# Seven block products for eight in the gates and in most of the down projection of a gated decoder layer

## The chip, the cores and the metric

The kernel runs on one core of a Trainium2 chip. A core has TensorE (PE) for matmuls, VectorE (DVE), ScalarE (ACT) and GpSimd (POOL) for elementwise work, and SyncE (SP), whose queue issues nearly all of this kernel's transfers to 16 DMA engines. The metric is the device time of one execution in microseconds; the median of several runs is given. Where a number comes from the profile, it is from one profiled execution.

## The reference, cut to what matters

One decoder layer on 2048 prompt positions and 64 sample positions, D = 1024, all in float32:

```python
h = rms_norm(x, pre_mix_g)
z = h @ w_in                                   # q, k, v, sg_u, sg_v, mq, gate_logits (3 x 1024)
branches = stack([attn, sg, memo])             # three branches of width 512
proj = einsum('blnc,ncd->blnd', branches, w_o)
gates = sigmoid(gate_logits.reshape(B, L, 3, 1024))
x = x + rms_norm(sum(gates * proj, axis=2), post_mix_g)
up = rms_norm(x, pre_ffn_g) @ w_up             # 1024 -> 2 * 2816
c = conv_b + sum(ext[:, j:j + L] * conv_w[j] for j in range(3))
act = gelu(gate half of c) * (value half of c)
x = x + rms_norm(act @ w_down, post_ffn_g)     # 2816 -> 1024
```

Beside the layer's output the caches and states are returned. The change touches what starts with `gate_logits` and ends with the down projection.

## The kernel before

Everything lies with channels on the 128 partitions and tokens along the free axis. The 2112 tokens form three groups of T2 = 704 columns (NG2 = 3), each of two chunks of CW = 352. Matmul operands are split (`split`, L72 and L73) into a high part in the fast float32 format and a low part that is the rest: ScalarE casts, VectorE subtracts. Each product is three passes (`PASSES`): high x high, high x low, low x high.

`stage1` computes the three branches and writes them to DRAM (`br`), as well as the scale of each token (`rbc_d`). `stage2` has three phases.

The mix phase (L789) goes over the three groups. `build_h` loads x, scales and splits it into eight operand tiles. `proj0` computes the group's first branch. `branches` then goes over the three branches n and four pairs of output tiles: per output tile 48 gate matmuls in `gemm` (L741, tile `ps_g`), a sigmoid (L872), and for n = 1 and 2 also 24 matmuls of the projection (tile `ps_p`), a product (L877) and a sum on GpSimd (L878). `SumSq` adds squares. After a group, the projection of the next group's first branch is issued, then `post_mix`: the norm of the sum (`rstd_rows`, with tiny matmuls on both sides of a power on GpSimd), scaling, the residual, a store of x1, squares and the norm of x1 itself, stored as `rs2_d` (L897).

After each pair of output tiles `prep` (L801) is called, for 22 up weight tiles in all: it loads four 128x512 blocks of the weight (L809), forms four sums and differences of them (L816), splits each and stores it to `sum_d` (L819). It has pools of its own.

The up phase (L913) multiplies in quads: two output tiles by two chunks by two halves of the depth, as seven block products in place of eight. `build_ops` loads x1, scales it, forms four differences per depth pair and splits seven operands; 28 operand tiles stand in 32 buffers. `build_w` loads three weight blocks and splits them, and loads four prepared sums. Each product is 12 matmuls (L997) into one of three kinds of PSUM bank. The last product of a quad is issued after the first one of the next.

The down phase (L1102) takes six chunks of 352 columns. Each loads and splits its 22 activation tiles (L1117), and per output tile two halves of the weight (L1125), with 66 matmuls (L1141, tile `ps_d`). Then come the norm, the scaling and the residual.

The order on each engine is a schedule made when the program is built: it goes by the order of the program, but an instruction that has its inputs and its buffer may be put ahead. The queues are then served in that order. Pools of a phase take the memory of the phase before, tile by tile as it falls free.

Of the kernel before, what the change touches and what calls it, by code (L numbers as in the profile page):

```python
# [15 lines left out]
P = 128  # L16
# [26 lines left out]
def tile_decoder_layer(ctx, tc, I, O):  # L43
# [8 lines left out]
    rs2_d = dpool.tile([P, NTOK], F32, tag="rs2d", name="rs2_d")  # L52
    sum_d = [dpool.tile([4, P, 2, 512], F32, tag=f"sumd{f}", name=f"sum_d{f}") for f in range(NF)]
# [46 lines left out]
    stage2(tc, I, O, br, rbc_d, x1_d, rs2_d, act_d, sum_d, gains, split, PASSES, rstd_rows)  # L100
# [609 lines left out]
def stage2(tc, I, O, br, rbc_d, x1_d, rs2_d, act_d, sum_d, gains, split, PASSES, rstd_rows):  # L710
# [3 lines left out]
    with ExitStack() as c2:  # L714

        def pool(stack, name, bufs):
            return stack.enter_context(tc.tile_pool(name=name, bufs=bufs, reuse_waits="tile"))

        cm = c2.enter_context(ExitStack())
        hp, wp, lp, sp = pool(cm, "h2", 13), pool(cm, "w2", 4), pool(cm, "ld2", 2), pool(cm, "s2", 2)  # L720

        def psum(stack, name):
            return stack.enter_context(tc.tile_pool(name=name, bufs=3, space=PSUM, reuse_waits="tile"))

        ps2 = psum(cm, "ps2")

        def load_w(src, nm):
            w = wp.tile([P, 2, 1024], F32R, tag="w", name=f"w_{nm}")
            t = lp.tile([P, 1024], F32, tag="ws", name=f"ws_{nm}", bufs=2)
            nc.sync.dma_start(out=t, in_=src)  # L730
            split(w[:, 0], w[:, 1], t)
            return w.rearrange("p s (k c) -> p s k c", c=P)

        def gemm(w, ks, xs, nm, spare=False):

            ps = ps2.tile([P, 2, 512], F32, tag="st" if spare else "mm", name=f"ps_{nm}", bufs=1 if spare else 3)
            n, tot = 0, 3 * len(xs)
            for k, x in zip(ks, xs):
                for a, b in PASSES:
                    for c in range(2):  # L740
                        nc.tensor.matmul(  # L741
                            ps[:, c, :CW], lhsT=w[:, a, k], rhs=x[:, b, c * CW : (c + 1) * CW],
                            start=(n == 0), stop=(n == tot - 1),
                        )
                    n += 1
            return ps[:, :, :CW]
# [42 lines left out]
def mix_phase(c2, tc, env):  # L789
# [7 lines left out]
    with ExitStack() as ca:  # L797
# [3 lines left out]
        def prep():  # L801

            if not todo:
                return
# [487 lines left out]
```

## Time and profile before

| | |
|---|---|
| median of 3 runs | 3159.44 us (3154.03 to 3162.03) |
| the profiled execution | 3162.45 us |
| its span | 3160.7 us |
| TensorE busy | 2996.0 us (95%) |
| VectorE, ScalarE, GpSimd busy | 1821.8, 1329.4, 547.0 us |
| DMA moved | 566.88 MB, mean 179 GB/s |

The profiled execution's span is what the rows below divide up; 1.75 us lie around it. A busy time is the sum of an engine's instructions, with overlaps counted once. Matmuls overlap, so one that is listed with 323 ns follows the one before it at about half of that; the pieces of the chain show the real pace. The share of DMA is the mean busy share of 16 engines.

### The profile page before, as it was taken

The numbers are of one execution on the slowest core, as the hardware profiler recorded it, in microseconds if no ns is written. First come the engines' busy times: TensorE is split into PE (matmuls) and PEld (weight loads), VectorE is DVE, ScalarE is ACT, GpSimd is POOL, SyncE is SP. The second block draws the span as 40 slices with busy tenths as digits, with TensorE's granted clock in tenths as the row PEclk, the third lists the DMA queues.
The fourth block names the chain that finished last, engine by engine and source line by source line (L and its number), as shares of the span: only waits on it lengthen the run. The fifth ranks groups of instructions, "written<-read, shape, count | busy, mean of one in ns | idle before, by whom it ended". The sixth has DMA issues, their size and how long they took to land.

```text
span 3160.7 us, 51575 instructions
## 1 busy us (share of the span) xinstructions
PE 2996.0 (95%) x20060; PEld 2950.8 (93%) x20060; DVE 1821.8 (58%) x3061; ACT 1329.4 (42%) x2371; POOL 547.0 (17%) x662
## 2 busy tenths in 40 slices
PE   8999999998999699989994999999999997999997
PEld 8899999998999699979994999999999997999997
DVE  6665766546656832462228665865586655555552
ACT  5555565114333422332213444544454444444441
POOL 3221100000011301130113101311132210222221
PEclk9999999999999799989996999999999998999999
DMA  6222223218787832252217777777777757666652
GB/s 201 62 61 82 88 86 105 64 48 313 261 276 246 295 131 86 88 177 67 72 46 253 250 246 244 266 245 244 240 262 245 240 174 255 219 223 216 208 187 100
DMA packets 245268, 566.88 MB, mean 179 GB/s; under 512 B 30672, under 2 KB 103888, under 8 KB 245008
## 3 DMA queue, kind: packets, MB, share of 16 engines
q1 hardware_dynamic: 245024, 563.59, 53.5%
q8 instruction: 158, 2.59, 0.3%
q14 instruction: 86, 0.70, 0.1%
HBM read 459.35 MB, written 105.13 MB: 179 GB/s over the span
## 4 chain that ended last, share of the span: by engine, by line
PE 78%; DMA 8%; DVE 7%; issue 3%; ACT 2%; POOL 1%; SPq 0%; DVEq 0%; ACTq 0%; POOLq 0%
PE ps_d L1141 16%; PE ps_x L997 16%; PE ps_g L741 11%; PE ps_y L997 8%; PE ps_p L741 4%; PE ps_w L997 4%; PE ps_q L189 3%; PE ps_up L203 3%; PE ps_sv L189 3%; DMA pr<-in_w_dram 3%; PE ps_mqp L203 3%; DMA sum_d<-pw 2%; PE ps_kv L189 1%; DVE m L891 1%; DVE pw L73 1%
## 5 line engine op out<-in xcount | busy, mean ns | idle before, releaser
L741 PE MATMUL ps_g<-h,w_g 128*128 128x352 f32 x3456 | 574.1, 326 | 18.6 <-ACT m L855 18.6
L741 PEld LDWEIGHTS ps_g<-h,w_g 128*128 128x128 f32 x3456 | 566.3, 191 | 19.1 <-ACT m L855 19.1
L1141 PE MATMUL ps_d<-a,wd 128*128 128x352 f32 x3168 | 512.5, 323 | 17.8 <-ACT a L72 17.1
L1141 PEld LDWEIGHTS ps_d<-a,wd 128*128 128x128 f32 x3168 | 508.6, 189 | 19.1 <-ACT a L72 17.7
L741 PE MATMUL ps_p<-b,w_p 128*128 128x352 f32 x1728 | 291.4, 326 | 18.6 <-ACT w_p L72 13.0
L741 PEld LDWEIGHTS ps_p<-b,w_p 128*128 128x128 f32 x1728 | 283.2, 191 | 20.3 <-ACT w_p L72 13.4
L1065 DVE SCALAR_TENSOR_TENSOR c<-e,k_conv_w,c 128x704 f32<-128x704 f32 (+1 forms) x264 | 252.1, 956 | 68.8 <-ACT c L1061 61.7
L73 DVE TENSOR_TENSOR wd<-wr,wd 128x1408 fp32r<-128x1408 f32 x96 | 161.4, 1685 | 206.1 <-ACT wd L72 204.6
L997 PE MATMUL ps_x<-ot,ws 128*128 128x352 f32 x1584 | 277.5, 323 | 0.6 <-ACT p L1006 0.5
L997 PEld LDWEIGHTS ps_x<-ot,ws 128*128 128x128 f32 x1584 | 258.4, 189 | 1.9 <-ACT p L1006 1.0
L73 DVE TENSOR_TENSOR wa<-ra,wa 128x512 fp32r<-128x512 f32 x198 | 134.9, 689 | 155.5 <-ACT wa L72 154.7
L878 POOL TENSOR_TENSOR m<-m,sg 128x704 f32<-128x704 f32 x48 | 98.2, 2045 | 709.6 <-DVE sg L877 495.1
L72 ACT CAST wd<-wr 128x1408 fp32r<-128x1408 f32 x96 | 131.8, 1372 | 109.1 <-PE ps_d L1141 90.7
L872 ACT ACTIVATE sg<-ps_g 128x704 f32<-128x704 f32 x72 | 54.5, 756 | 284.4 <-PE ps_g L741 284.3
L1061 ACT ACTIVATE c<-e,k_conv_b,k_conv_w 128x704 f32<-128x704 f32 (+1 forms) x132 | 129.6, 982 | 68.8 <-DVE e L1031 49.0
L997 PE MATMUL ps_x<-ob,wa 128*128 128x352 f32 x792 | 147.3, 326 | 11.7 <-ACT wa L72 7.4
L72 ACT CAST wa<-ra 128x512 fp32r<-128x512 f32 x198 | 121.8, 624 | 85.9 <-PE ps_y L997 46.2
L73 DVE TENSOR_TENSOR w_g<-ws_g,w_g 128x1024 fp32r<-128x1024 f32 x72 | 98.7, 1371 | 91.9 <-ACT w_g L72 89.3
L1052 POOL COPY tails<-e 128x2 f32<-128x2 f32 x88 | 61.4, 697 | 520.6 <-DVE e L1031 520.4
L997 PE MATMUL ps_w<-ob,wa 128*128 128x352 f32 x792 | 147.9, 323 | 0.7 <-ACT wa L72 0.7
L997 PE MATMUL ps_y<-ot,ws 128*128 128x352 f32 x792 | 146.7, 324 | 0.3 <-DMA ws<-sum_d 0.3
L997 PEld LDWEIGHTS ps_x<-ob,wa 128*128 128x128 f32 x792 | 131.7, 191 | 12.5 <-ACT wa L72 7.6
(304 smaller groups left out, 5037.3 us busy)
## 6 DMA issues: line engine op xcount, KB each, us to landing
ws<-sum_d SPq DMA_DIRECT2D x264, 512.0 KB, 5.1
wr<-in_w_dram SPq DMA_DIRECT2D x96, 704.0 KB, 4.1
ra<-in_w_dram SPq DMA_DIRECT2D x198, 256.0 KB, 3.8
sum_d<-pw SPq DMA_DIRECT2D x88, 512.0 KB, 5.0
ws_g<-in_w_dram SPq DMA_DIRECT2D x72, 512.0 KB, 4.0
af<-act_d SPq DMA_DIRECT2D x132, 176.0 KB, 4.1
pr<-in_w_dram SPq DMA_DIRECT2D x88, 256.0 KB, 5.0
ws_p<-in_w_dram SPq DMA_DIRECT2D x36, 512.0 KB, 3.3
```

The source lines that it names most:

```text
L72: nc.scalar.copy(out=hi, in_=src)
L73: nc.vector.tensor_tensor(out=lo, in0=src, in1=_f(hi), op=ALU.subtract)
L189: nc.tensor.matmul(ps[:nt, :256], lhsT=h[k // 4][:, a, k % 4, c0 : c0 + nt], rhs=wv[:, b, k], start=(n == 0), stop=(n == 3 * KT - 1),)
L203: nc.tensor.matmul(ps[:, :nt], lhsT=wv[:, a, k, half * P : (half + 1) * P], rhs=h[k // 4][:, b, k % 4, :nt], start=(n == 0), stop=(n == 3 ...
L741: nc.tensor.matmul(ps[:, c, :CW], lhsT=w[:, a, k], rhs=x[:, b, c * CW : (c + 1) * CW], start=(n == 0), stop=(n == tot - 1),)
L872: nc.scalar.activation(v2(sg), ps, AF.Sigmoid)
L878: nc.gpsimd.tensor_tensor(out=mx[o], in0=mx[o], in1=sg, op=ALU.add)
L997: nc.tensor.matmul(ps[:, :CW], lhsT=self.ws[w][:, a, j], rhs=self.ops[o][j][:, b], start=(start and n == 0), stop=(n == 3 * HK - 1), skip_ ...
L1052: nc.gpsimd.tensor_copy(out=tails[:, ft], in_=e[:, T2 : T2 + 2])
L1061: nc.scalar.activation(c[:, :cwid], e[:, 2:ew], AF.Identity, bias=cb[:, ft : ft + 1], scale=cw[:, ft, 2:3])
L1065: nc.vector.scalar_tensor_tensor(out=c[:, :cwid], in0=e[:, t : t + cwid], scalar=cw[:, ft, t : t + 1], in1=c[:, :cwid], op0=ALU.mult, op1= ...
L1141: nc.tensor.matmul(ps[:, :CW], lhsT=w[:, a, k], rhs=acts[i * HF + k][:, b], start=(n == 0), stop=(n == 3 * NF - 1),)
```

## The change

The gates get a phase of their own ahead of the mix phase. It computes all 36 pairs of gate output tiles as quads of seven products, as the up phase does, and stores the sigmoids to DRAM (`sg_d`). In group 0 the sums of a gate weight are formed on the spot, used and stored; in groups 1 and 2 they are loaded. The up weights' sums are prepared there too, after each quad of groups 1 and 2 until the 22 are done, in the pools of the quads.

The mix phase then has the projections alone, and loads the gate tiles. `post_mix` of a group is issued after the second pair of output tiles of the next group. It stores the sums of squares of x1 (`acx_d`) in place of the finished norm; `norms` in the up phase makes the norm from them, for the next group at f = 8.

The down phase takes whole groups. 16 of the 22 depth tiles go in two batches of eight through seven-product quads that add into the output tiles `ys`; the other six go plainly (`plain`), and the norm and the residual of a group are held until after the next group's first quad. The eight down weights' sums are prepared in the up phase, one after each fourth quad. The quad code of the up phase has become the class `Strassen`, which all three phases use; `rw` has 10 buffers in the gate phase and 5 in the up phase as before, `wo` has 12 and in the down phase 10.

The diff's core:

```diff
+        def weights(self, w, sums, first, nm):
...
+            def total(i):
+                if ("s", i) not in raw:
+                    p, m, op = (
+                        (lambda: block(2), lambda: block(3), ALU.add),
+                        (lambda: block(0), lambda: block(2), ALU.subtract),
+                        (lambda: total(0), lambda: block(0), ALU.subtract),
+                        (lambda: block(1), lambda: total(2), ALU.subtract),
+                    )[i]
+                    p, m = p(), m()
+                    t = rw.tile([P, HK * P], F32, tag="raw", name=f"s{i}_{nm}")
+                    nc.vector.tensor_tensor(out=t, in0=p, in1=m, op=op)
+                    raw["s", i] = t
+                return raw["s", i]
...
+                t = wo.tile([P, 2, HK * P], F32R, tag="w", name=f"w{n}_{nm}")
+                if n[0] == "a":
+                    split(t[:, 0], t[:, 1], block(i))
+                elif first:
+                    split(t[:, 0], t[:, 1], total(i))
+                    nc.sync.dma_start(out=sums[i], in_=_f(t))
                 else:
+                    nc.sync.dma_start(out=_f(t), in_=sums[i])
...
+        def run(self, jobs):
+            prev = None
+            for nm, ws, ops, sink in jobs:
+                q = [nm, ws, ops, sink, {}]
+                p1 = self.copy(q, self.product(q, "x", "a11", "b11", True), "p1")
+                if prev:
+                    self.end(prev)
+                p5 = self.copy(q, self.product(q, "y", "s1", "t1", True), "p5")
+                sink.add(0, 0, p1, self.product(q, "w", "a12", "b21", True))
+                u2 = self.copy(q, self.product(q, "x", "s2", "t2", False), "u2")
+                sink.add(0, 1, u2, self.product(q, "y", "s4", "b22", False))
+                sink.half(0)
+                u3 = self.copy(q, self.product(q, "x", "s3", "t3", False), "u3")
+                sink.add(1, 1, u3, p5)
+                prev = q
+            self.end(prev)
...
+def gate_phase(c2, tc, env):
...
+    op_, wo, rw = pool(c2, "ops", 32), pool(c2, "wo", 12), pool(c2, "raw", 10)
+    lp, gp, cp = pool(c2, "ldu", 3), pool(c2, "sg", 4), pool(c2, "cp", 8)
+    eng = Strassen(ps2, op_, wo, rw, cp, lp)
...
+        def half(self, h):
+            part = chunk(self.sg[h], 1) if h else self.sg[h]
+            nc.scalar.activation(part, part, AF.Sigmoid)
+            nc.sync.dma_start(out=sg_d[2 * self.i + h][:, self.g * T2 : (self.g + 1) * T2], in_=self.sg[h])
+    def jobs():
+        todo = list(range(NF))
+        for g in range(NG2):
+            c0 = g * T2
+            rb = lp.tile([P, T2], F32, tag="rb", name=f"rb_{g}", bufs=1)
+            nc.sync.dma_start(out=rb, in_=rbc_d[:, c0 : c0 + T2])
+            ops = eng.operands(lambda k: I["xT"][:, k, c0 : c0 + T2], f"h{g}", 0, rb)
+            for i in range(12):
+                yield f"g{g}_{i}", eng.weights(I["wg"][i], sum_d[NF + i], g == 0, f"g{g}_{i}"), ops, Sink(g, i)
+                if g and todo:
+                    f = todo.pop(0)
+                    eng.weights(I["w3"][f], sum_d[f], "sums", f"u{f}")
...
+def mix_phase(c2, tc, env):
...
+        nc.sync.dma_start(out=acx_d[g], in_=acx)
...
+                    sg = gp.tile([P, T2], F32, tag="sg", name=f"sl_{g}_{n}_{o}")
+                    nc.sync.dma_start(out=sg, in_=sg_d[8 * n + o][:, g * T2 : (g + 1) * T2])
+                    if n == 0:
+                        m = mp.tile([P, T2], F32, tag="m", name=f"m_{g}_{o}")
+                        nc.vector.tensor_tensor(out=v2(m), in0=v2(sg), in1=ps[:, :, :CW], op=ALU.mult)
...
+                if held and n == 0 and op == 1:
+                    post_mix(*held)
+                    held = None
+        held = g, mx, acc
+    post_mix(*held)
...
 def up_phase(c2, tc, env):
...
+    def norms(g):
+        rb = lp.tile([P, T2], F32, tag="rb", name=f"rb2_{g}", bufs=1)
+        acc = ep.tile([P, E_W], F32, tag="e", name=f"acx_{g}")
+        nc.sync.dma_start(out=acc[:, :T2], in_=acx_d[g])
+        for c in range(2):
+            psb = ps2.tile([P, 512], F32, tag="st", name=f"ps_su{g}_{c}", bufs=1)
+            cols = slice(c * CW, (c + 1) * CW)
+            rstd_rows(acc[:, cols], CW, psb[:, CW:], lambda c0, w: psb[:, c0 : c0 + w], kp, f"u{g}_{c}")
+            nc.vector.tensor_copy(out=rb[:, cols], in_=psb[:, :CW])
+        return rb
...
+                yield f"u{g}_{f}", eng.weights(I["w3"][f], sum_d[f], False, f"u{g}_{f}"), ops, Sink(g, f)
+                if f % 4 == 3 and 5 * g + f // 4 < 8:
+                    i = 5 * g + f // 4
+                    eng.weights(I["w4s"][i], sum_d[NF + 12 + i], "sums", f"d{i}")
+                if f == 8 and g + 1 < NG2:
+                    rb = norms(g + 1)
...
 def down_phase(c2, tc, env):
...
+        put(0, 0, eng.product(q, "x", "a11", "b11", True))
+        if end:
+            end()
+        put(1, 1, eng.product(q, "y", "s1", "t1", True))
+        add(0, 0, eng.product(q, "w", "a12", "b21", True))
+        put(0, 1, eng.product(q, "x", "s2", "t2", False))
+        add(0, 1, eng.product(q, "y", "s4", "b22", False))
+        add(1, 1, eng.product(q, "x", "s3", "t3", False))
+        return lambda: put(1, 0, eng.product(q, "x", "a22", "t4", False))
...
+    for g in range(NG2):
+        ys = []
+        for b in range(NB):
+            ops = eng.operands(lambda k: act_d[8 * b + k][:, g * T2 : (g + 1) * T2], f"d{g}_{b}", None, None)
+            for op in range(4):
...
+                end = quad(nm, ws, ops, ys[2 * op : 2 * op + 2], b == 0, end)
+                if held:
+                    final(*held)
+                    held = None
+        acts = load_acts(g)
+        acc = sp.tile([P, T2], F32, tag="acc", name=f"acc_{g}")
+        if g + 1 < NG2:
+            plain(g, acts, ys, (0, 1), acc, end)
+            held, end = (g, ys, acc, (0, 1)), None
+        else:
+            plain(g, acts, ys, (0,), acc, end)
+            plain(g, acts, ys, (1,), acc, lambda: final(g, ys, acc, (0,)))
+            final(g, ys, acc, (1,))
```

## Rows read from the trace of the kernel before

**Rows 1.** The page: TensorE's busy time, and the chain's shares by engine.

```profile
PE 2996.0 (95%) x20060; PEld 2950.8 (93%) x20060; DVE 1821.8 (58%) x3061; ACT 1329.4 (42%) x2371; POOL 547.0 (17%) x662
PE 78%; DMA 8%; DVE 7%; issue 3%; ACT 2%; POOL 1%; SPq 0%; DVEq 0%; ACTq 0%; POOLq 0%
```

**Rows 2.** Chain in order of time, mix phase: start us, us, what.

```profile
1165.91 7.76 PE ps_g L741 x48
1173.67 3.88 PE ps_p L741 x24
```

**Rows 3.** The same chain in the up phase, pieces that open two quads.

```profile
1906.53 5.45 PE ps_x L997 x34
1919.99 5.12 PE ps_x L997 x32
```

**Rows 4.** The same chain in the down phase, two chunks.

```profile
2722.69 80.03 PE ps_d L1141 x500
2808.73 80.05 PE ps_d L1141 x500
```

**Rows 5.** Tile ps_p: count, ns min/median/max, first and last start us, forms.

```profile
L741 PE MATMUL ps_p<-b,w_p x1728: 317/323/661, 731.5 to 1647.6; 128*128 128x352 f32 x192
```

**Rows 6.** Busy time by stretch, columns as headed; last three clock, DMA share, GB/s.

```profile
core 0: us, PE busy (x) PEld busy (x) DVE busy (x) ACT busy (x) POOL busy (x), PEclk, DMA share, GB/s
726.00:746.00 20.00, 14.54 (x79) 14.54 (x80) 14.24 (x17) 11.54 (x16) 0.00 (x0) 0.77 1.02 388
731.00:764.00 33.00, 32.53 (x190) 32.54 (x191) 24.76 (x30) 19.13 (x26) 0.00 (x0) 0.93 0.93 337
764.00:1050.00 286.00, 280.00 (x1726) 278.49 (x1725) 181.79 (x222) 115.55 (x159) 34.54 (x16) 0.99 0.77 270
1050.00:1110.00 60.00, 31.96 (x184) 31.38 (x184) 52.49 (x54) 23.63 (x33) 24.67 (x10) 0.72 0.81 281
1347.00:1416.00 69.00, 53.48 (x318) 52.90 (x318) 49.77 (x44) 27.27 (x35) 23.28 (x11) 0.83 0.53 173
1416.00:1650.00 234.00, 231.93 (x1436) 231.63 (x1435) 63.12 (x59) 49.40 (x58) 30.63 (x16) 1.00 0.20 65
1703.00:1727.00 24.00, 18.55 (x83) 17.14 (x84) 17.37 (x35) 11.74 (x27) 0.00 (x0) 0.75 0.92 339
1727.00:2013.00 286.00, 286.00 (x1785) 285.69 (x1785) 187.88 (x274) 144.02 (x258) 44.24 (x86) 1.00 0.75 251
2013.00:2031.00 18.00, 16.96 (x102) 15.87 (x101) 16.46 (x30) 10.48 (x23) 5.93 (x2) 1.00 0.83 290
2606.00:2630.00 24.00, 6.48 (x25) 5.63 (x24) 11.14 (x12) 9.25 (x12) 0.00 (x0) 0.64 0.95 348
```

**Rows 7.** DMA issues: what, queue, count, KB each, median us to landing.

```profile
sum_d<-pw SPq DMA_DIRECT2D x88, 512.0 KB, 5.0
pr<-in_w_dram SPq DMA_DIRECT2D x88, 256.0 KB, 5.0
act_d<-c SPq DMA_DIRECT2D x44, 352.0 KB, 5.1
```

**Rows 8.** Tile pr, its loads on SP's queue: columns as in rows 5.

```profile
L809 SPq DMA_DIRECT2D pr<-in_w_dram x88: 327/425/2357, 698.1 to 1113.3; - x88
```

**Rows 9.** Groups by line and shape: count, busy us, mean ns, idle before, releaser.

```profile
L73 DVE TENSOR_TENSOR wa<-ra,wa 128x512 fp32r<-128x512 f32 x198 | 134.9, 689 | 155.5 <-ACT wa L72 154.7
L72 ACT CAST wa<-ra 128x512 fp32r<-128x512 f32 x198 | 121.8, 624 | 85.9 <-PE ps_y L997 46.2 <-PE ps_w L997 24.0 <-PE ps_x L997 7.8
L816 DVE TENSOR_TENSOR pr<-pr,pr 128x512 f32<-128x512 f32 x88 | 62.1, 706 | 55.3 <-DMA pr<-in_w_dram 54.6
L73 DVE TENSOR_TENSOR ot<-t,ot 128x352 fp32r<-128x352 f32 x48 | 24.7, 518 | 0.0
L951 DVE SCALAR_TENSOR_TENSOR ux<-ux,c_gains,rb 128x704 f32<-128x704 f32 x24 | 22.6, 946 | 10.0 <-DMA ux<-x_d 8.7 <-DMA rb<-rs_d 1.2
```

**Rows 10.** Timeline, TensorE at the start of the mix phase: start, us, what.

```profile
731.47 33.04 PE L741 MATMUL ps_p<-b,w_p 128*128 128x352 f32 x192 [12.64 <-ACT w_p L72]
```

More of the change, by code (lines that the diff above doesn't have):

```diff
@@ L945, in build_ops, with pool, v2, chunk @@
+    def pool(stack, name, bufs):
+        return stack.enter_context(tc.tile_pool(name=name, bufs=bufs, reuse_waits="tile"))
+    def v2(t):
+        return t.rearrange("p (c n) -> p c n", c=2)
+    def chunk(t, c):
+        return t[:, c * CW : (c + 1) * CW]
+    class Strassen:
+        def __init__(self, ps, op_, wo, rw, cp, lp):
+            self.pools = ps, op_, wo, rw, cp, lp
+        def operands(self, xs, nm, gain, rb):
+            _, op_, _, _, _, lp = self.pools
             ops = {n: [] for n in ("b11", "t1", "b21", "t2", "b22", "t3", "t4")}
@@ L965, in build_ops, with block @@
             return ops
-        def build_w(f, nm):
+        def weights(self, w, sums, first, nm):
+            _, _, wo, rw, _, _ = self.pools
+            raw = {}
+            def block(i):
+                if i not in raw:
+                    raw[i] = rw.tile([P, HK * P], F32, tag="raw", name=f"r{i}_{nm}")
+                    nc.sync.dma_start(out=raw[i], in_=w[:, i * 512 : (i + 1) * 512])
+                return raw[i]
+            def total(i):
[11 more added lines that the diff above has]
+                return raw["s", i]
+            if first == "sums":
+                for i in range(4):
+                    total(i)
@@ L978, in build_w @@
-                ws[n] = w.rearrange("p s (k c) -> p s k c", c=P)
-            return ws
-        class Quad:
-            def __init__(self, g, f, ops):
-                self.g, self.f, self.nm, self.ops = g, f, f"{g}_{f}", ops
-                self.ws = build_w(f, self.nm)
-                self.ps = {}
-            def product(self, bank, w, o, start):
-                if start:
-                    self.ps[bank] = ps2.tile(
-                        [P, 512], F32, tag="q" + bank, name=f"ps_{bank}{self.nm}", bufs=3 if bank == "x" else 2
-                    )
-                ps, n = self.ps[bank], 0
-                for j in range(HK):
+                if first == "sums" and n[0] == "a":
+                    continue
@@ new lines, in end, with product @@
+        def end(self, q):
+            q[3].move(1, 0, self.product(q, "x", "a22", "t4", False))
+            q[3].half(1)
+        def product(self, q, bank, w, o, start):
+            nm, ws, ops, _, banks = q
+            if start:
+                banks[bank] = self.pools[0].tile(
+                    [P, 512], F32, tag="q" + bank, name=f"ps_{bank}{nm}", bufs=3 if bank == "x" else 2
+                )
+            ps, n = banks[bank], 0
+            for j in range(HK):
+                for a, b in PASSES:
+                    nc.tensor.matmul(
+                        ps[:, :CW], lhsT=ws[w][:, a, j], rhs=ops[o][j][:, b],
+                        start=(start and n == 0), stop=(n == 3 * HK - 1), skip_group_check=True,
+                    )
+                    n += 1
+            return ps[:, :CW]
```

679 lines of the change are left out of this document (305 added, 374 removed).

## The prediction, made before the changed kernel was run

> **What bounds the kernel now.** I read the page's busy shares and chain first, then the chain in order of time, then busy time by stretch. TensorE is busy 95% of the span and carries 78% of the chain [rows 1]; where it runs undisturbed the pieces repeat exactly. In the mix phase 48 gate matmuls take 7.76 us and 24 projection matmuls 3.88 us [rows 2]: 161.7 ns each. In the up phase a quad of 84 matmuls starts every 13.46 us [rows 3]: 160.2 ns each. In the down phase a chunk of 528 takes 86.04 us [rows 4], 1.4 us more than 528 x 160.2 ns. So removed matmuls are worth their whole 160 ns, if nothing else becomes late.
>
> The mix phase runs from 731.5 to 1647.9 us [rows 5], 916.4 us, for 5184 matmuls that need 838.3: 78 us are lost. Nearly all of it lies in two stretches, 1050-1110 and 1347-1416 [rows 6]: of the 184 and 318 matmuls there 64 each are the tiny ones of the norms, so 19 and 41 us of real products fill 60 and 69 us. There post_mix and the norm of x1 stand between two groups, with the granted clock down to 0.72 and 0.83. The second resource is DMA. While the preparation of the up weights runs (764-1050), its engines are at 0.77 share and 270 GB/s, afterwards at 0.20 (1416-1650) [rows 6].
>
> **Gates: the matmuls.** 72 outputs x 7.76 = 558.7 us become 36 quads x 13.46 = 484.6 us [rows 2, 3]; the projections keep 72 x 3.88 = 279.4 us. That is 74 us less, on the path.
>
> **Gates: the transfers.** In MB (KB of 1024), from the sizes in [rows 7]: a 512-column weight block is 0.262, a split sum 0.524, a 704-column row tile 0.360. A quad of group 0 loads four blocks, stores four sums and two gate tiles: 3.87 MB in 13.46 us. With 3.2 MB of operands that makes 307 GB/s over the group, which just fits. A quad of groups 1 and 2 loads three blocks and four sums and stores two tiles: 3.60 MB. To 22 of these 24 quads the change adds one preparation of an up weight: four blocks in, four sums out, 3.15 MB. Such a quad moves 6.75 MB; in 13.46 us that would be 501 GB/s, more than any stretch shows. Groups 1 and 2 move 22 x 6.75 + 2 x 3.60 + 2 x 3.24 = 162.2 MB. They last as long as that takes, and not 24 x 13.46 = 323 us.
>
> The rate decides everything. Where TensorE did not pace the loads, the engines gave 337 GB/s at 0.93 share (731-764), 339 at 0.92 (1703-1727), 348 at 0.95 (2606-2630) and, for 20 us, 388 at full share (726-746) [rows 6]. Three of the four lie at 337 to 348; the fourth holds old preparations, loads of weights and of rows together, much as the new quads will. I take 350, just above the three: 162.2 / 0.350 = 463 us. Bounds: 388 GB/s gives 418 us; 270 GB/s, the preparation's own stretch (764-1050), gives 601 us. The old preparation was cheap because its 88 loads were spread over 415 us of TensorE work [rows 8] and its tiles had pools of their own. Now its tiles rotate through the pools of the quads' weights, and its stores stand on SP's queue in front of the next quad's loads. A store that waits for its split holds those loads, and TensorE waits for them.
>
> VectorE does not take over: a quad has 7 splits of 0.69, 4 sums of 0.71 and 3 adds of 0.52 us [rows 9], 9.2 us. ScalarE has 7 casts of 0.62 us [rows 9], three copies and three sigmoids. Both stay under 13.46 us.
>
> The Trainium skill weighs on this rate (HBM Reference, Specifications (TRN2)): a core that streams alone measures about 425 GB/s, bounded by its 16 DMA engines, while its share with both cores of a pair busy is about 358. By 425 groups 1 and 2 would take 382 us, by 358 453 us. The trace passes the lower figure in 726-746 (388 for 20 us) and nowhere nears the higher one for that long; it does not decide between them.
>
> **New seams.** Start: the first product needs operands of four depth pairs. Each pair is two scalings, four differences and seven splits on VectorE, about 7.6 us ([rows 9]; 0.95 for a scaling). The old phase needed four plain splits and ran at full speed from 731.47 on, after a gap of 12.64 us [rows 10]. The same build at the start of the up phase ran 83 matmuls (13.3 us) in 24 us (loss 10.7); the start of the down phase ran 25 in 24 us (loss 20) [rows 6]. I take 14, between those two. Gates to mix: branch tiles and weights wait for memory of the last quad, 0 to 20 us; I take 12, near the 12.64 us of the old seam [rows 10]. Group 0 at 307 GB/s: 3 us, bounds 0 and 22 (49.6 MB at 270 GB/s are 184 us).
>
> **post_mix behind the next group's first products; norms in the up phase.** TensorE now has the next group's projections under post_mix. The 24 row loads and 24 stores of x1 go to SP between weight loads, at a low demand. The norms' matmuls still wait in TensorE's order for GpSimd's power, with the products queued behind. In the down phase the same chain costs 1.4 us per chunk [rows 4], so I take 3 us per group, 9 in all, in place of the 78 lost before; bounds 0 and those 78. The last post_mix stays uncovered. Its chain of the x1 norm goes, and a norm for group 0 comes in front of the up operands: zero, plus or minus 10.
>
> **Up phase.** Eight preparations of down weights, one in four quads: 251 GB/s x 53.8 us is 13.5 MB, and 3.15 more make 309 GB/s, under 350, so they are mostly hidden: 1.5 us each. Uncovered, 3.15 MB at 350 GB/s is 9 us each, 72 in all. Their eight raw tiles share five buffers with the quads, and the quads' own loads queue behind on SP. Two norms inside at 3 us: 18 us together, bounds 0 and 78.
>
> **Down phase.** 24 quads x 13.46 + 864 x 0.1602 = 461.5 us against 6 x 86.04 = 516.2 us. Eight further builds of operands: at the up phase's change of group 102 matmuls (16.3 us) filled 18 us [rows 6], so 2 us each, 16. The plain tiles with two weight buffers and the norms: 6. Together 483.5, 33 less; bounds 461.5, and 548 at 10.7 us per build. The cover is VectorE: per four quads 44 operand steps, 28 adds and 12 splits, 45.6 of 53.8 us [rows 9]. If it falls behind, a PSUM bank is read late and TensorE waits: about 1 us a quad, 24 us.
>
> **The sum.** Gates and mix: 14 + 161.5 + 3 + 463 + 12 + 279.4 + 9 = 942 us against 916.4: +25.5. Up +18, down -33. Net +10.5 us on the span of 3160.7 us, which is 3171. The profiled execution (3162.45 us) lies 3.0 us over the median of the runs, its span 1.3 us over it, so the median becomes 3170 us.
>
> **Rivals.** (A) The engines keep up: once TensorE does not pace the demand they hold 388 GB/s, as in 726-746 [rows 6]. Groups 1 and 2 take 418 us and the time is 3125: faster. It decides from 366 GB/s (443 us) on. For it: that window has the same sorts of transfer. Against it: the windows of 24 to 33 us at 337 to 348, two of them with as much demand.
>
> (B) SP's order holds the loads back: a preparation's stores wait for load (5.0 us to landing [rows 7]), sum, cast and split, and the share stays near the 0.77 of 764-1050. Between 337 and 270 GB/s groups 1 and 2 take 481 to 601 us: 3188 to 3308.
>
> (C) Preparations in the up phase or builds in the down phase are not covered: some 70 us more, 3240.
>
> (D) No change that can be told, as a stretch of the forecast: 351 to 366 GB/s, 3160 give or take 9.5. A measurement of this kernel tells about 0.3%, which is those 9.5 us.
>
> **How the numbers follow.** Forecast (337 to 366 GB/s, 3150 to 3188) 0.45, of which 0.20 is D; A 0.30; B 0.20; C 0.05. Faster is A, 0.30; same is D, 0.20; slower is the rest of the forecast with B and C, 0.50. Both signs hold much of the chance, so the likeliest case's own range stands beside the wide one: 3150 to 3188. The wide one leaves out what passes 395 GB/s and what falls under 297: 3115 to 3255.
>
> **What would show it.** In gate groups 1 and 2: DMA share over 0.9 and some 19 us per quad with a preparation in place of 13.46, TensorE's longest waits on loads of sums or on weights behind them, its granted clock under 1 after gaps (as 0.75 in 1703-1727 [rows 6]). Group 0 at about 13.5 us a quad. Mix groups back to back at 3.88 us per tile. The up phase some 18 us longer, the down phase some 33 shorter. Wrong is the forecast if groups 1 and 2 run at 13.5 to 17 us or over 21 us per quad, or if the preparations move into another stretch, where the old kernel leaves room (0.20 share in 1416-1650 [rows 6]).

## The result, and the profile after

The changed kernel takes 3240.38 us (median of 4 runs), the kernel before 3159.76 (4 runs of the same job): a ratio of 1.0258, 95% interval 1.0240 to 1.0276, slower. The profiled span is 3238.8 us, 78.1 more than before. The stages, by the first and last starts of their matmuls:

| stage | before | after | difference | predicted |
|---|---|---|---|---|
| until the first matmul of gates or mix | 731.5 | 728.2 | -3.3 | 0 |
| gates and mix | 916.1 | 981.4 | +65.3 | +25.5 |
| last mix matmul to last up matmul | 958.2 | 975.1 | +16.9 | +18 |
| last up matmul to last down matmul | 535.7 | 525.6 | -10.1 | -33 |
| from there to the end | 19.2 | 28.5 | +9.3 | not in the sum |

After, the page's line of TensorE's busy time, the answer to [rows 1] (the other engines follow on it):

```profile
PE 2943.3 (91%) x19340; PEld 2863.3 (88%) x19340; DVE 2066.1 (64%) x3859; ACT 1407.1 (43%) x2767; POOL 443.9 (14%) x583
```

TensorE has 53 us less to do and the span is 78 us longer, so 131 us more of it are idle. After, tiles of the gates, the mix and the up phase (line, engine, what, count: ns min/median/max, first to last start in us; forms). Gates run from 728.2 to 1409.8, the mix to 1709.6; [rows 5] is the line of before:

```profile
L836 PE MATMUL ps_xg<-ob_h,wa_g x432: 317/326/663, 728.2 to 1380.4; 128*128 128x352 f32 x144
L970 PE MATMUL ps_p<-b,w_p x1728: 317/325/662, 1409.8 to 1709.6; 128*128 128x352 f32 x192
L836 PE MATMUL ps_xu<-ob_u,wa_u x792: 317/323/659, 1775.3 to 2670.4; 128*128 128x352 f32 x198
L836 PE MATMUL ps_xu<-ot_u,wa_u x792: 317/323/427, 1811.8 to 2684.7; 128*128 128x352 f32 x198
```

After, busy time by stretch (columns as in [rows 6]): the start of the gates, gate groups 1 and 2, the start of the down phase, its two changes of group.

```profile
728.00:762.00 34.00, 22.16 (x66) 16.93 (x67) 34.00 (x65) 16.43 (x35) 0.00 (x0) 0.60 0.72 248
911.00:1404.00 493.00, 380.56 (x2039) 354.03 (x2037) 226.18 (x387) 191.27 (x369) 0.00 (x0) 0.91 0.86 320
2686.00:2726.00 40.00, 19.92 (x82) 16.11 (x83) 27.50 (x56) 18.93 (x41) 0.00 (x0) 0.74 0.82 291
2886.00:2926.00 40.00, 31.55 (x191) 31.25 (x190) 28.91 (x48) 13.59 (x29) 1.00 (x1) 0.87 0.76 267
3050.00:3090.00 40.00, 31.55 (x194) 31.26 (x194) 26.89 (x44) 11.46 (x24) 1.00 (x1) 0.87 0.71 243
```

The second line is the case. 493 us for 24 quads that TensorE could do in 323; no engine is near its limit (VectorE 226, ScalarE 191 of 493), and the DMA engines are idle for 14% of the time although TensorE waits for weights. A quad with a build lasts (493 - 2 x 13.46) / 22 = 21.2 us. Who waits for whom from 945 to 1380 says where the idle time comes from. TensorE, then SP's own queue (total us, times, longest):

```profile
PE ps_xg L836 <- ACT wa_g L73: 78.0, 18, 7.2
SPq L880 <- ACT sg L879: 123.2, 18, 8.8
SPq L799 <- DVE ws_u L74: 19.4, 23, 3.5
```

TensorE waits for the cast of the next quad's weights, and SP stands at line 880, the store of the sigmoids, until this quad's sigmoids are made. (SPq is SP's queue.) One such wait in order of time on SP's queue (start us, us, instruction):

```profile
1049.99 2.84 SPq L770 DMA_DIRECT2D r_u<-in_w_dram  x3
1061.58 0.33 SPq L880 DMA_DIRECT2D sg_d<-sg  x1
1062.01 0.38 SPq L799 DMA_DIRECT2D sum_d<-ws_u  x1
1062.44 2.19 SPq L770 DMA_DIRECT2D r_g<-in_wg_dram  x3
```

From 1052.8 to 1061.6 SP issues nothing. The three weight blocks of the next quad leave only behind the store, at 1062.4, and TensorE's next quad begins at 1067.8. But a wait does not prove a cause: with engines that are full anyway, the loads would land no sooner. That is what the runs had to tell apart.

### The profile page after: what moved, and what is told of

Read it like the earlier page. It is cut to its first block, busy times and chain, and to the rows that moved or that the text cites. A ratio compares the mean times of both kernels' runs of the same rounds, so it can differ in the third digit from the quotient of the medians.

```text
span 3238.8 us, 52272 instructions
## 1 busy us (share of the span) xinstructions
PE 2943.3 (91%) x19340; PEld 2863.3 (88%) x19340; DVE 2066.1 (64%) x3859; ACT 1407.1 (43%) x2767; POOL 443.9 (14%) x583
## 4 chain that ended last, share of the span: by engine, by line
PE 76%; DMA 9%; DVE 6%; issue 3%; ACT 2%; POOL 1%; SPq 1%; POOLq 0%; DVEq 0%; ACTq 0%
PE ps_xu L836 15%; PE ps_yu L836 7%; PE ps_p L970 7%; PE ps_xd L836 6%; PE ps_xg L836 5%; PE ps_wu L836 4%; PE ps_p L1180 4%; PE ps_yg L836 3%; PE ps_q L190 3%; PE ps_up L204 3%; PE ps_yd L836 3%; DMA ws_g<-sum_d 3%; PE ps_sv L190 3%; PE ps_mqp L204 2%; PE ps_kv L190 1%
## 5 line engine op out<-in xcount | busy, mean ns | idle before, releaser
L836 PE MATMUL ps_xu<-ot_u,ws_u 128*128 128x352 f32 x1584 | 278.1, 323 | 0.2 <-ACT u_u L845 0.2
L836 PEld LDWEIGHTS ps_xu<-ot_u,ws_u 128*128 128x128 f32 x1584 | 258.5, 189 | 0.9 <-ACT u_u L845 0.9
L836 PE MATMUL ps_xg<-ot_h,ws_g 128*128 128x352 f32 x864 | 152.0, 324 | 4.4 <-DMA ws_g<-sum_d 3.7
L836 PE MATMUL ps_wu<-ob_u,wa_u 128*128 128x352 f32 x792 | 150.3, 325 | 2.5 <-ACT ob_u L73 1.5
L836 PE MATMUL ps_xu<-ob_u,wa_u 128*128 128x352 f32 x792 | 148.1, 326 | 4.8 <-ACT ob_u L73 3.7
L836 PE MATMUL ps_yu<-ot_u,ws_u 128*128 128x352 f32 x792 | 148.6, 326 | 0.3 <-ACT ot_u L73 0.3
L836 PEld LDWEIGHTS ps_xg<-ot_h,ws_g 128*128 128x128 f32 x864 | 140.1, 189 | 8.3 <-issue 7.8
L1180 PE MATMUL ps_p<-a,wd 128*128 128x352 f32 x864 | 142.9, 325 | 4.5 <-DVE wd L74 3.2
L1180 PEld LDWEIGHTS ps_p<-a,wd 128*128 128x128 f32 x864 | 140.0, 190 | 5.6 <-DVE wd L74 3.8
L836 PE MATMUL ps_yu<-ob_u,ws_u 128*128 128x352 f32 x792 | 138.9, 322 | 0.0
```

Of the source, the lines that this page charges most:

```text
L836: nc.tensor.matmul(ps[:, :CW], lhsT=ws[w][:, a, j], rhs=ops[o][j][:, b], start=(start and n == 0), stop=(n == 3 * HK - 1), skip_group_chec ...
L1180: nc.tensor.matmul(ps[:, :CW], lhsT=w[:, a, k], rhs=acts[k][c][:, b], start=(n == 0), stop=(n == 3 * ND - 1))
```

## The experiments

"Gate phase" is the time from the first gate matmul to the first projection. Groups 1 and 2 are that less 188.6 us: group 0 with its start 183, and 5.6 from there to the first projection, as in the changed kernel. In the other runs that last seam is up to 3 us shorter or 4 us longer. Share and GB/s are those of the trace over groups 1 and 2; the trace holds 3 to 6% fewer bytes than the count, by which the expectations go.

| run | edit | median us | gate phase | groups 1, 2 | share | GB/s |
|---|---|---|---|---|---|---|
| after | | 3240.4 | 681.6 | 493 | 0.86 | 320 |
| e1 | sigmoid stores off SP | 3241.3 | 684.7 | 496 | 0.87 | 318 |
| e2 | no builds | 3071.1 | 518.1 | 330 | 0.79 | 268 |
| e5 | all stores of the stretch off SP | 3196.6 | 637.4 | 449 | 0.94 | 351 |
| e6 | half the bytes per sum | 3213.7 | 655.2 | 467 | 0.82 | 289 |
| e9 | e5 and e6 together | 3147.8 | 590.0 | 401 | 0.93 | 337 |
| e7 | 11 builds in stage 1 | 3153.1 | 565.9 | 377 | 0.88 | 326 |
| e11 | stores off SP, 14 builds here | 3131.1 | 563.7 | 375 | 0.95 | 354 |
| e10 | stores off SP, 8 builds here | 3108.9 | 530.4 | 342 | 0.90 | 326 |

### e1: the sigmoid stores on ScalarE's queue

```diff
-            nc.sync.dma_start(out=sg_d[2 * self.i + h][:, self.g * T2 : (self.g + 1) * T2], in_=self.sg[h])
+            nc.scalar.dma_start(out=sg_d[2 * self.i + h][:, self.g * T2 : (self.g + 1) * T2], in_=self.sg[h])
```

> The changed kernel with one edit: the stores of the sigmoid results leave from ScalarE's own queue, not from SP's. In the gate groups 1 and 2 of the changed kernel (911 to 1404 us, 493 us for 162.2 MB, 329 GB/s, DMA share 0.87) SP stood 123 us behind these stores, 18 waits of up to 8.8 us each, with the next quad's loads queued behind them. Theory 'order': the loads were held back by that, the engines could give the 380 GB/s that they gave elsewhere, so the two groups take about 427 us and the kernel about 3175 us. Theory 'bytes': the engines are at their limit and SP's waits are only the place where the lack shows; the two groups stay at 485 to 500 us and the kernel at 3235 to 3245 us, and SP's waits move to other instructions.

Measured 3241.32 us (3236.21 to 3245.85). Not one microsecond came of taking the longest wait away. SP's waits in the same stretch, this kernel:

```profile
SPq L799 <- DVE ws_u L74: 174.8, 58, 9.6
```

The next store in line, that of the builds' sums, had been waiting behind the sigmoid's; now it does the holding. Taken by itself this run speaks for "bytes"; with e5 below it only shows that one of two stores was not enough.

### e2: no builds in the gate phase

```diff
-                if g and todo:
-                    f = todo.pop(0)
-                    eng.weights(I["w3"][f], sum_d[f], "sums", f"u{f}")
...
-                yield f"u{g}_{f}", eng.weights(I["w3"][f], sum_d[f], False, f"u{g}_{f}"), ops, Sink(g, f)
+                yield f"u{g}_{f}", eng.weights(I["w3"][f], sum_d[NF + f % 12], False, f"u{g}_{f}"), ops, Sink(g, f)
```

> The changed kernel without the 22 builds of the up weights' sums in the gate phase; the up projection loads the gate weights' sums in their place (same bytes), so what it computes is not the up projection. 69.2 MB of the 162.2 MB of gate groups 1 and 2 are gone, 93 MB are left. Theory 'bytes': the groups become bound by TensorE, 24 quads of 13.46 us or 323 us at 288 GB/s, so 170 us less, about 3070 us. Theory 'order': the sigmoid stores still stand in SP's queue ahead of the next quad's loads, so part of the loss stays; the groups take 360 to 400 us, the kernel 3110 to 3150 us.

Measured 3071.05 us, the number of theory 'bytes'. From 911 to 1241 us (this kernel) TensorE is busy for 327 of 330 us at full clock:

```profile
911.00:1241.00 330.00, 327.06 (x2040) 326.49 (x2038) 120.44 (x215) 137.36 (x281) 0.00 (x0) 1.00 0.79 268
```

So the builds are the whole loss of groups 1 and 2 (163 us), and the quads by themselves cost what the prediction said. The sigmoid stores alone hold nothing that matters. How the builds cost it, by their bytes, by their stores in the queue or by their work on the engines and in the pools, is still open here.

### e5: every store of the stretch off SP's queue

e1's edit, and in `weights`, for the builds of the up weights:

```diff
-                    nc.sync.dma_start(out=sums[i], in_=_f(t))
+                    (nc.gpsimd if first == "sums" and nm[0] == "u" else nc.sync).dma_start(out=sums[i], in_=_f(t))
```

> The changed kernel with every store of the gate groups 1 and 2 taken off SP's queue: the sigmoid results leave from ScalarE's queue, the up weights' sums from GpSimd's. With only the sigmoid stores moved, the two groups took the same 493 us and SP stood 175 us behind the sums' stores (58 waits, up to 9.6 us) where it had stood 123 us behind the sigmoid stores. In this kernel only loads are left on SP. Theory 'bytes': the 16 DMA engines carry what they can, 0.87 of their time busy; the groups stay at 480 to 500 us, the kernel at 3230 to 3250 us. Theory 'order': a store that waits for another engine holds the loads, whichever store it is; the groups take about 427 us (380 GB/s), the kernel about 3175 us.

Measured 3196.56 us (3194.44 to 3197.04): 44 us less with the same bytes and the same arithmetic. Busy time from 945 to 1230, the changed kernel and then this one:

```profile
945.00:1230.00 285.00, 212.15 (x1122) 196.27 (x1121) 130.53 (x222) 108.66 (x210) 0.00 (x0) 0.90 0.88 326
```

```profile
945.00:1230.00 285.00, 229.54 (x1251) 217.00 (x1251) 144.18 (x247) 117.51 (x233) 30.82 (x58) 0.90 0.96 360
```

Who holds whom now, in this kernel from 945 to 1330: the builds' stores wait on GpSimd's queue, where nothing stands behind them.

```profile
POOL sum_d L799 <- DVE ws_u L74: 348.7, 60, 14.0
SPq L770 <- DMA ws_g<-sum_d: 62.3, 31, 5.0
SPq L770 <- DVE s_u L783: 59.4, 27, 5.1
```

Neither theory got its number (427 or 480 to 500; it is 449), because both hold one after the other: the order of SP's queue cost 44 us, and with it gone the DMA engines are at 0.96 share and 360 GB/s. That is near their end: in proportion, 351 GB/s at 0.94 share is 373 at full share, and the changed kernel's 320 at 0.86 is 372. So the engines moved the bytes no faster than before; what was won is time in which they stood idle. Two things remain on SP: 62.3 us of waits behind the loads of sums and 59.4 us of loads that wait for a buffer until a build's sum (`s_u`) is formed. What the shared buffers cost was not tried by itself. The Trainium skill (HBM Reference, Specifications (TRN2)) gives about 425 GB/s for a core that streams alone and about 358 as its share with the pair's other core busy; these runs, on one core, come to 351 to 360 over 285 us and more, at 0.94 to 0.96 share, nearer to the lower figure.

The Trainium skill (DMA: Bandwidth & Descriptors, Issuing engines are not separate DMA queues) says that starting transfers from several engines only saves the short time that it takes to start them. e5 agrees in so far as the rate at full share stays the same, and differs in what was saved: 44 us, because a start that waits no longer stood ahead of starts that could go.

### e6 and e9: half the bytes, with the stores on SP and off it

For the builds of the up weights, with e2's second edit beside it (the up phase loads other sums):

```diff
-                    nc.sync.dma_start(out=sums[i], in_=_f(t))
+                    nc.sync.dma_start(out=sums[i][:, 0], in_=_f(t[:, 0]))
```

> The changed kernel with the same number of instructions and of stores in the same queues, but each store of an up weight's sum carries half (the rounded part; the rest is not stored, and the up projection loads the gate weights' sums in their place, so it does not compute the up projection). 23.1 MB of the 162.2 MB of gate groups 1 and 2 are gone, 139.1 MB are left. Theory 'bytes': 139.1 MB at 329 GB/s are 423 us, so 70 us less, about 3170 us. Theory 'work or order': the builds' instructions on VectorE and ScalarE and the waits in SP's queue stand as they did, so 480 to 500 us for the groups and 3228 to 3245 us for the kernel.

> The two edits that each gave only a part, together: the stores of the gate groups 1 and 2 off SP's queue (sigmoid results on ScalarE's, the up weights' sums on GpSimd's), and half the bytes in each store of an up weight's sum (the up projection loads the gate weights' sums instead, so it does not compute the up projection). With the stores off SP the two groups moved 162.2 MB in about 449 us (361 GB/s, DMA share 0.96); with half the bytes but the stores on SP they took about 467 us for 139.1 MB (298 GB/s, share 0.82). Theory 'queue first, bytes behind it': with the queue free the groups go by bytes, 139.1 MB at 361 GB/s are 385 us, 64 us less than with the stores off SP alone: about 3132 us. Rival 'work': the builds' own instructions hold the quads and bytes count for little; 26 us less, as in the kernel with half the bytes alone: about 3170 us.

e6 measured 3213.7 us, 27 less; e9, with e5's edit on top, 3147.78, 92.6 less. 23.1 MB fewer are worth 27 us while SP holds the loads and 48.8 once it doesn't. With SP's order in the way the rate even fell (289 GB/s at 0.82 share): the stores in the queue were as many, and from 945 to 1380 SP waited 219 us for what they carry, against 172 in the changed kernel. "Bytes" expected 70 of the first run, "work or order" none; the second was expected at 3132 and missed by 16: 139.1 MB in 401 us are 347 GB/s by count, where I had taken 361. TensorE is busy 354 of 402 us there, so the limits begin to share.

### e7: 11 builds moved into stage 1

```diff
+    room = wp.tile([P, 2, KT * 256], F32R, tag="w", name="room")    # the fifth weight buffer, free in the second pass
...
+        prep(room, 1 + (i in (3, 6)))    # per token block: four loads, sums on GpSimd, split, four stores
...
-                if g and todo:
+                if g and i % 2 and todo:
```

> The changed kernel with 11 of the 22 builds of the up weights' sums moved into the second pass of the first stage (the nine token blocks before 728 us, where the DMA share was 0.24), with the additions on GpSimd, in a weight buffer that is free there; the other 11 stand behind every second quad of the gate groups 1 and 2. 34.6 MB leave the two groups, 127.6 MB are left. Theory 'bytes': 127.6 MB at 329 GB/s are 388 us, 105 us less, and the first stage grows by 0 to 15 us: 3135 to 3150 us. Theory 'order': each build that is left still costs its 8 us in SP's queue, 24 quads of 13.46 us and 11 times 8 us are 411 us, 82 us less: 3158 to 3173 us.

Measured 3153.05 us (10 runs), a ratio of 0.9985 (0.9976 to 0.9995) to the kernel before: no change worth the name, and between the two theories. The gate phase fell by 115.7 us, more than either theory gave; but stage 1 grew by 27.8 us, where I had taken 0 to 15. The builds were scheduled at once when the buffer fell free, not one per block: their 44 stores left between 485 and some 640 us, 14 us a build. Busy time from 540 to 600, the changed kernel and then this one.

```profile
540.00:600.00 60.00, 59.20 (x492) 58.73 (x493) 32.67 (x60) 12.81 (x26) 3.15 (x8) 1.00 0.30 77
```

```profile
540.00:600.00 60.00, 48.27 (x366) 47.17 (x366) 49.27 (x69) 18.52 (x34) 28.80 (x22) 0.86 0.85 283
```

### e3: the norm of x1 behind the mix again

In `post_mix`, where `psb` is a new PSUM tile; of `norms(g)` in the up phase only the load of `acx_d` is left:

```diff
+        rstd_rows(
+            acx, T2, psb[:, 0, CW:], lambda c0, w: psb[:, c0 // CW, c0 % CW : c0 % CW + w], sp, f"u{g}"
+        )
+        nc.vector.tensor_copy(out=v2(acx), in_=psb[:, :, :CW])
         nc.sync.dma_start(out=acx_d[g], in_=acx)
```

> The changed kernel with the norms of x1 made again behind each group's mix, as before the change; the up phase only loads the result. The seam from the last mix matmul to full speed in the up phase was 79 us before and 90 us after the change, with SumE idle 39.9 us until the sums of squares arrived. Theory: the two norms at the start of the up phase (matmul, power, broadcast, copy, about 3 us each) and their load cost 8 to 14 us, so about 3226 to 3232 us. Rival: the load only stood late in SP's queue behind the stores of x1, and stands as late in this version, while the third norm of each group makes the mix stage longer by 3 to 9 us: 3238 to 3246 us.

("SumE" is TensorE.) Measured 3234.08 us (3232.06 to 3237.72), 6.3 less, between the two. The long wait in the changed kernel, and the two that stand there in this one (TensorE, 1705 to 1810):

```profile
PE ps_su L85 <- DMA acx<-acx_d: 39.9, 1, 39.9
```

```profile
PE ps_su L85 <- DVE acx L933: 26.7, 1, 26.7
PE ps_su L95 <- POOL rstd_u L92: 13.8, 1, 13.8
```

The idle time is nearly the same under other names. From the first mix matmul to the first sum product of the up phase (full speed) it is 389.0 us in the changed kernel (1409.8 to 1798.8) and 389.3 here (1410.5 to 1799.8): nothing was won up to there. What was won is 4.6 us inside the up phase (885.9 to 881.3), so about 2.3 us for each of the two norms there. From the last mix matmul to full speed it was 76.1 us before the change, 89.2 after it and 78.8 here: the norm's place accounts for 10 of those 13 us, but the mix pays for it, being 10.7 us longer.

### e4: the gate part alone, with the down projection as before

> One part of the change alone: gates by seven products, norms in the up phase, but the down projection as before (22 depth tiles plainly, no sums of down weights built in the up phase). By the two traces the new down phase took 10.2 us less between the first and the last down matmul and 9.3 us more behind the last, and the 8 builds in the up phase showed as no idle time of TensorE. Theory: the down part is worth 0 to -5 us, so this kernel takes 3238 to 3246 us. Rival: the builds in the up phase or their stores cost 10 to 17 us that stand as the up phase's growth, so this kernel takes 3222 to 3232 us.

The edit puts `down_phase`, the layout of `w4` and an up phase without the eight builds back. Measured 3240.64 us (3237.13 to 3243.44): the down part is worth nothing that can be told. This is where the theory had it. The eight builds cost 2 us in the up phase (907.4 against 909.4), and from the last up matmul to the end the old phase takes 557.4 us, the new one 554.1.

### e8: x1 earlier in the down phase

```diff
+            xs = xfirst(g, (0, 1))    # blocks 0 and 1 of x1, ahead of the plain products
             plain(g, acts, ys, (0, 1), acc, end)
...
+            xs = xfirst(g, (1,))      # last chunk: six blocks of x1 into the three tiles of the operand loads
             plain(g, acts, ys, (1,), acc, lambda: final(g, ys, acc, (0,)))
```

> The changed kernel with x1 for the last addition of the down phase loaded earlier: the first two blocks of each of the first two token groups ahead of its plain products, and six of the eight blocks of the last chunk into three load buffers that are free there. In the changed kernel 28.2 us lay behind the last matmul (18.9 us before the change), with the additions waiting about 3.5 us for each pair of loads into two buffers, and 17 us of TensorE's idle time at the two group changes, behind the stores of the held blocks. Theory 'late x1': the tail falls by 8 to 12 us and the group changes by 4 to 10 us: 3218 to 3228 us. Rival: the tail and the changes are set by VectorE's own 16 operations of about 1 us and by the stores, and the loads were only late by the same measure: 3234 to 3244 us.

Measured 3229.9 us (3228.85 to 3232.3), 10.5 less, between the two; 9.2 of it came at the end: 19.3 us from the last matmul's start to the end in place of 28.5. The waits that went (3205 to 3240, changed kernel):

```profile
POOL y L1210 <- DMA xf<-x_d: 13.5, 3, 6.5
DVE y L1210 <- DMA xf<-x_d: 10.1, 5, 3.5
```

At the changes of group the rival was right: both kernels have, word for word, this line.

```profile
PE ps_xd L836 <- ACT y L1136: 16.9, 2, 8.4
```

There the first copy into a new block waits for one of ten buffers, of which the held group still has eight: at 2904.9 us it goes after 6.9 us of waiting for a store of the held blocks. Whether x1 was there earlier did not matter.

### e10, e11 and e12: versions put together

e10 has the edits of e3, e5 and e8, and a place for each build: 8 of 22 in stage 1, each tied to its token block by a small copy from that block's activation into the load's target; 8 behind every third quad of gate groups 1 and 2; 6 in the mix. e11 has 14 in the gates and none in the mix, e12 8 in the gates, 14 in the mix and none in stage 1.

```diff
+                    nc.gpsimd.tensor_copy(out=a[i][:, 0:1], in_=late)     # stage 1: late = uT[:, 0, 0:1]
                     nc.sync.dma_start(out=a[i], in_=I["w3"][f][:, i * 512 : (i + 1) * 512])
...
+            w = lp.tile([P, 2, 512], F32R, tag="pw", name=f"pw_{f}_{i}", bufs=1)     # mix: one output buffer
```

> A version put together from the runs: the stores of gate groups 1 and 2 off SP's queue; of the 22 builds of the up weights' sums 8 stay behind every third quad there, 8 stand in the second pass of the first stage, one behind each of the first eight token blocks (each held until that block's activation is there), 6 in the mix phase outside the norms; the norms of x1 behind each mix again; x1 loaded early in the down phase. Gate groups 1 and 2 carry 118 MB, at 361 GB/s 327 us, about what TensorE needs (323 us). Theory 'queue first, bytes behind it': 493 to 330 us, the norms 6 us and the down phase 10 us less, the first stage 5 to 15 and the mix 0 to 15 us more: about 3079 us (3065 to 3095). Rival: the builds collide in the first stage and in the mix as 11 of them did in the first stage (28 us): 3100 to 3130 us.

> The same version with the 6 builds of the mix phase back in gate groups 1 and 2: 14 builds there, 137.1 MB. Theory 'queue first, bytes behind it': 137.1 MB at 361 GB/s are 380 us, 50 us more than with 8 builds, and the mix gets back what the 6 builds cost there (0 to 15 us): 3110 to 3135 us, 35 to 50 us above the version with the 6 in the mix. Rival 'work': 14 builds hide as well as 8 once the stores are off SP, within 15 us of the other.

e10 measured 3108.91 us (3103.3 to 3112.89), a ratio of 0.9842 (0.9823 to 0.9860) to the kernel before, 131 us under the changed kernel: 1.6% faster than the kernel before, and clear of the noise. The time is the rival's (3100 to 3130), not the theory's (3065 to 3095). The gate phase is 12 us over what was expected, with groups 1 and 2 at TensorE's pace (busy 331 of 342 us):

```profile
932.00:1274.00 342.00, 331.00 (x2035) 327.03 (x2034) 157.36 (x275) 152.80 (x310) 17.29 (x32) 1.00 0.90 326
```

The rest was lost where the rival had it: stage 1 is 20.6 us longer (8 builds, 2.6 each, as in e7: 2.5) and the mix 19 us, of which e11 shows 12.5 without any build there, and e3 10.7 by its norm alone. e11 measured 3131.11 us (3124.56 to 3135.7); it is 22 us above e10, where 35 to 50 were expected; the gate phases themselves are 33.3 us apart, and the mix, without builds, gives 6.5 back.

> The version with the builds spread over three places (3109 us), with the 8 builds of the first stage moved to the mix phase: 14 there, 8 in gate groups 1 and 2, none in the first stage. In the spread version the first stage was 20.6 us longer for 8 builds (2.6 us each) and the mix 6.5 us longer for 6 (1.1 us each, against the version without them). Theory 'a build costs what the place has left': the first stage gives back 18 to 21 us, the mix carries 44 MB beside its own 62 MB in about 310 us (340 GB/s, below the 361 GB/s of the gates) and grows by 8 to 16 us: 3096 to 3108 us. Rival: the mix runs into the DMA engines' limit and VectorE's (0.73 busy there without builds, 0.25 us of it more for each us): it grows by 30 to 50 us, 3118 to 3140 us.

e12 measured 3197.55 us (3194.4 to 3200.53): 89 over e10, and worse than the rival, for a reason that neither had. Stage 1 gave back its 20 us and the mix itself grew by 4.5 us only (323.3 against 318.8). Then TensorE stands still ahead of the up phase (waits of TensorE, 1580 to 1775, and of SP, 1580 to 1745; then one build's four stores, and the first of the next, in SP's order of time):

```profile
PE ps_xu L836 <- ACT wa_u L73: 101.8, 2, 101.5
SPq L977 <- DVE pw L74: 104.0, 27, 7.1
```

```profile
1662.52 0.32 SPq L977 DMA_DIRECT2D sum_d<-pw  x1
...
1666.87 0.32 SPq L977 DMA_DIRECT2D sum_d<-pw  x1
...
1671.20 0.32 SPq L977 DMA_DIRECT2D sum_d<-pw  x1
...
1675.53 0.32 SPq L977 DMA_DIRECT2D sum_d<-pw  x1
...
1681.56 0.32 SPq L977 DMA_DIRECT2D sum_d<-pw  x1
```

With one output buffer the next split waits until the last store has landed (ScalarE's casts wait 68.5 us for that here): 4.3 us each, 19 us a build. In the mix itself builds went slower still: 24 stores, those of six builds, in 276 us, as in e10 (270 us); so the mix grew little. The other eight builds ran behind it, from 1584 to 1733, and their stores stand in SP's queue ahead of the first loads of the up phase, which leave from 1733 on. The DMA engines are at 0.53 share meanwhile. As in the gate groups of the changed kernel, stores that wait have loads behind them. More output buffers were not tried.

## Why the prediction was right or wrong

The side was right (slower), and the time lies in the wide range; but that range took in rates down to 297 GB/s, and the likeliest case, 3150 to 3188, did not come. Its place was taken by rival B, whose time was to be 3188 to 3308 and whose mark (over 21 us per quad) was named as what would make the forecast wrong. Of the 70 us between forecast and result, groups 1 and 2 of the gates account for 30 and the down phase with its tail for 32; group 0 and the mix add 5 and 11, and the seam between gates and mix and the first stage take 6 and 3 off.

**The rate in groups 1 and 2** is the first step that failed: 463 us forecast at 350 GB/s, 493 measured at 329 by the same count of bytes. The 350 was read from stretches of 20 to 33 us [rows 6], in which SP waited at most 4.7 us for a build's store. As a price of the engines it was good: e5 moves the same 162.2 MB in 449 us, 361 GB/s. What was missing is that the queue must let the engines have their work. The mechanism stood in the text ("its stores stand on SP's queue in front of the next quad's loads"), yet it got a case of 0.20 and no term in the sum. Its price is 44 us (e5). The stretch 764-1050, 270 GB/s at 0.77 share [rows 6], was used as a bound of the rate, but TensorE was busy for 280 of its 286 us: it shows what was asked for, and prices neither the engines nor the queue. What it could have shown is SP standing behind the old builds' stores, with little harm there (before, 764 to 1050):

```profile
SPq L819 <- DVE pw L73: 96.2, 53, 7.9
```

B named the builds' stores alone; at first the sigmoid's store stood in front, and e1 shows that either holds the loads.

**Gates, TensorE's part**: right. e2's 330 us for 24 quads are 13.7 a quad, where 13.46 [rows 3] was taken.

**The start of the gates**: 14 us predicted, 23.4 measured, outside its bound of 20: 66 matmuls, 10.6 us of work, fill the 34 us from 728 to 762, and VectorE is busy for all of them. The operands were the price, as said, but group 0 also splits its first weights there. **Group 0** as a whole took 183 us, 21.5 over its 161.5, so its own 3 us for bytes did not show. **Gates to mix**: 12 predicted, 5.6 measured.

**The mix**: 279.4 + 9 predicted, 299.8 measured, 20.4 lost in place of 9. 8.7 of it are two waits of TensorE (the first line; the second is the seam ahead of the mix, from the end of the last gate product):

```profile
PE ps_p L970 <- DVE m L979: 8.7, 2, 4.3
PE ps_p L970 <- ACT w_p L73: 7.2, 1, 7.2
```

These two are `post_mix` on VectorE with the next group's products behind it, the cover that was priced at 3 us a group. About 6 are the norms' tiny matmuls between the products, and 2 the first 30 us of the mix, at a granted clock of 0.92; the rest was not followed. The greater part of the 78 us lost before is gone, as said.

**The up phase**: +18 predicted, +17 measured, and right by chance. Eight builds cost 2 us (e4), where 12 was taken, two norms 4.6 (e3), where 6 was taken; from full speed on the phase grew by 3.8 us in all. The other 13 us came at the seam ahead of it, which had been put at 0, give or take 10.

**The down phase**: 33 less predicted, 0.8 less measured with its tail. This is the second step that failed. Two terms were mis-sized. A change of operands inside the phase was put at 2 us, from the up phase's change [rows 6]; at the two changes of group 191 and 194 matmuls (30.6 to 31.1 us) fill 40 us, 9 each, because blocks of the group before still hold the buffers. The start lost 27 us where that of before lost 20 [rows 6]. And the tail was in no term at all: 9.3 us, which e8 gives back by loading x1 of the last chunk earlier.

**The rivals.** A (engines keep up at 388 GB/s) came in no run: with the queue free the 162.2 MB took 449 us, 361 GB/s by count, only 6 us above the 443 from which A would have decided (e5). C, some 70 us in the up phase or the down phase, did not come: the up phase's builds cost 2 us (e4), and the new down phase is no longer than the old, though 32 us short of its forecast. The last mark of the prediction, that builds elsewhere would change the outcome, is what e7 and e10 show.

## What to carry to other kernels

Where one queue issues both loads and stores, a store that waits for compute can hold the loads behind it (44 us in e5); ask of each store that a change adds what is queued behind it, and if two kinds of store can wait, move both before judging. A measured rate is the engines' only if the queue was not held and the loads were asked for in time. Here the held queue showed as a DMA share of 0.82 to 0.87 beside a TensorE that waited for weights (e6, after, e1); with the queue free it was 0.94 (e5). Work that is "covered by an idle resource" must also end before its stage does: count its chain per piece, buffers included (e12).

## What the runs showed of the hardware that I had not expected

The busiest wait in the profile may be worth nothing alone: 123 us of SP's waiting moved to the next instruction in the queue (175 us there), with 0.9 us of change in the time (e1). Two causes in a row gave more together than the sum of each alone: 27 us by half the bytes, 44 by the queue, 92.6 by both (e6, e5, e9). And a build of the same bytes cost 7.4 us among the gates with stores on SP (163 us for 22, e2), 2.6 in the first stage (e10), and almost nothing in the up phase (2 us for eight, e4).
